# Sums of squares in two float32r products in place of two float32 products

## The chip, the cores and the metric

The kernel runs on one core of one Trainium2 chip. The metric is the device time of one execution in microseconds (us); lower is better. One profiled execution of the kernel before gives the rows that are quoted below.

## What is computed

A two-layer transformer block on 256 image tokens x and 256 context tokens (1024 features, float32), followed by a second block of two hybrid layers on x alone and a last norm. Cut to what matters here:

```python
def _rmsnorm(h, g):
    hf = h.astype(jnp.float32)
    hf = hf * lax.rsqrt(jnp.mean(hf * hf, axis=-1, keepdims=True) + NORM_EPS)
    return hf.astype(h.dtype) * g

def _modulate(h, shift, scale):
    return h * (1 + scale) + shift

# each sublayer of the first block, for x and for the context:
#   u = modulate(rmsnorm(h, g_pre), shift, scale)
#   y = sublayer(u)          # feed-forward, or an attention with its output product
#   h = h + factor * gate * rmsnorm(y, g_post)
# sublayers in order: ffn, differential attention, ffn | ffn, neighbourhood attention, ffn
```

So every sublayer needs two root-mean-squares per token for each half of the tokens: one of its output y, one of the new h. In the second block there are further norms over 256 features (MLA's c_q), over 128 features (c_kv, the heads of the attentions) and a last one over 1024.

## The kernel before

**Layout.** Features lie on the 128 partitions, tokens along the free dimension: h is a tensor of 128 partitions, 8 feature tiles, 512 tokens (x in 0 to 255, the context in 256 to 511). A sum over the features of a token is therefore a sum over 8 tiles and then over the partitions; the second one is a product with a matrix of ones on TensorE, which leaves the sum in every partition of a PSUM bank (tile `n`).

**Products.** Weights and activations are float32. `split` holds an operand as two float32r parts: ScalarE copies it into `hi`, VectorE subtracts that from it into `lo`. `mm3` makes each product in three passes of float32r. Weights arrive by DMA from the queue of SyncE (tile `raw`), are split (line 155 on ScalarE, line 156 on VectorE, tile `w`, 128x1024 each), and there are buffers for four split weights. TensorE's own work is one long queue of these passes.

**Sums of squares.** `Sums` (lines 54 to 81) takes four parts of 128 x 2 x 256 numbers. ScalarE squares a part (line 64, tile `r`, 128x512); VectorE adds parts 2 and 3 to part 1 (line 62, 128x512); with part 4, VectorE folds the sum of the first three and then part 4 itself to 128x256 (line 62, two instructions), and both 128x256 tensors go as a list to `rstd`. There (line 348, made by line 164 in `mm`) two float32 products with ones, 256 columns each, add them over the partitions. Then ScalarE takes the table's inverse root (line 353) and VectorE makes one Newton step of three instructions (lines 354 to 356). With `direct`, used where only x is left, the four squared parts go to TensorE in eight float32 products instead; the change leaves that as it is.

**Where the sums stand.** `link` (line 1348) joins two sublayers for one half of the tokens: `rstd` of y's sums, `add_normed` (lines 375 and 379: h += factor * y * r), `norm_r` (the sums of the new h), and `normed` (lines 413 to 421: the next input u, four tiles, each as hi and lo). For x, `link` stands behind the last products of x (`xdone`), and the context's last products of the same sublayer are there for TensorE meanwhile. For the context, `link` is the `mid` of the next sublayer, and TensorE has that sublayer's products of x meanwhile: two features (`AHEAD`) of the first feed-forward, five features of the second and third, or x's values and first queries and keys in an attention. There are four such joints with both halves (ffn to attention, attention to ffn, ffn to ffn, ffn to attention), which makes eight links of two sums each; before them stand the first norm of x (in `ada_first`) and of the context. Those are 18 sums that are not `direct`.

`rstd` is called with one 128x256 tensor in two more places of each hybrid layer (lines 1186 and 1195, the norms of c_q and c_kv; four in all): one float32 product each. With 512 columns it is called in the attentions, and that path stays.

**Order.** A scheduler orders the instructions of each engine beforehand: those that come first in the program go first, as soon as by its own estimate their operands and a buffer are there. On the chip each engine then runs its queue in that order and waits at the head of it. The 128x512 tiles of tag `r512` have two buffers.

Of the kernel before, what the change touches and what calls it, by code (L numbers as in the profile page):

```python
# [32 lines left out]
FA = 12  # L33
# [10 lines left out]
class Split:  # L44
    """A float32 operand held exactly as the sum of two float32r parts."""
# [8 lines left out]
class Sums:  # L54
    """sums of squares over the 1024 features of 256 tokens, from four parts [128, 2, 256]: the parts added
    up on the vector engine or, direct, on the tensor engine"""
# [3 lines left out]
    def add(self, x):  # L60
# [5 lines left out]
        if self.direct:  # L66
            if self.n == 1:
                self.acc = net.nps.tile([128, 512], F, name="n", tag="n")[:, :256]
            for t in range(2):
                net.mm(self.acc, net.ones, s[:, t], self.n + t == 1, self.n + t == 5)  # L70
        elif self.n == 1:
            self.acc = s
        elif self.n < 4:
            tt(self.acc, s)
        else:
            for x in (self.acc, s):
                tt(x[:, 0], x[:, 1])
            self.acc = [self.acc[:, 0], s[:, 0]]
# [5 lines left out]
class Net:  # L84
# [16 lines left out]
    @contextmanager  # L101
    def psum(self, **tags):
        """The PSUM banks of a phase: a number for each kind of use."""
        with ExitStack() as es:
            self.banks = self.pool(es, "ps" + "_".join(tags), 1, space=bass.MemoryType.PSUM)
            self.nbank = tags
            yield

    @contextmanager
    def space(self, name, n):  # L110
        """The 4 KiB tiles of a phase."""
# [4 lines left out]
    # ---- tiles  # L116
# [21 lines left out]
    # ---- weights: raw float32 from DRAM, then two float32r parts that sum to it  # L138
# [19 lines left out]
    # ---- products. A start clears the flags of its whole bank. Groups that share a bank are run one  # L158
    # after another (groups=0), or as one group (groups=n) whose first matmul alone has the start and
    # whose last alone the stop.  # L160
# [28 lines left out]
    # out += stat^T @ mov for every (out, mov), in three passes of float32r  # L189
# [12 lines left out]
    # ---- constants  # L202
    def setup(self):
        nc, I = self.nc, self.I
        self.ones = self.const([128, 128], "ones")
# [24 lines left out]
    # ---- modulation vectors: ada_w^T silu(c) + ada_b, as columns  # L230
    def ada_first(self):
        """The first layer's first scale and the last quarter of its shift on the tensor engine, the rest of
        the shift on the vector engine. Returns x's norm factors."""
# [45 lines left out]
    def ada_chunks(self, l, mods):  # L279
        """Thunks, one for each 128 values of modulation, and one for each vector that adds the bias."""  # L280
# [31 lines left out]
    def spread(self, thunks, steps):  # L312
        """An iterator: each next() runs its share of the thunks."""
# [11 lines left out]
    # ---- norm factors as columns  # L325
    def pre_cols(self, l, which, j):
        """(1 + scale) * g and shift of sublayer `which` (0, 1, 2) for half j."""
# [11 lines left out]
    # ---- 1 / sqrt(sum of squares / n + eps) in every partition: a table's value and one Newton step  # L339
    def rstd(self, ss, n, p=None):  # L340
        """ss: tensors whose sum is to be summed over the partitions, if p, that sum in PSUM, isn't given"""
        nc = self.nc
        if p is None:
            ss = ss if isinstance(ss, list) else [ss]
            w = ss[0].shape[-1]
            p = self.nps.tile([128, 512], F, name="n", tag="n")[:, :w]
            for i, x in enumerate(ss):
                self.mm(p, self.ones, x, i == 0, i == len(ss) - 1)
            v = ss[-1]
# [17 lines left out]
    def add_normed(self, y, r, cols, j):  # L367
        """h += cols * rmsnorm(y), y in two tiles [128, 4, 256]"""
# [12 lines left out]
    def table(self, x):  # L381
        """loads the table of the inverse root, once x is there"""
        self.nc.scalar.activation(self.col.tile([128, 1], F, name="tb", tag="tb", bufs=1), x, AF.Abs_reciprocal_sqrt)

    def new_u(self, n=2):
        """hi and lo of [1024, 256 n] features by tokens"""
# [16 lines left out]
    def normed(self, u, cols, shift, j, r=None, dve=False):  # L403
        """u = rmsnorm(h) * cols + shift in two parts"""
# [18 lines left out]
    def scaled(self, cols, shift=None):  # L423
        """h * cols of x in two parts, with shift's parts in the two columns that follow, if there is one, and
        the factors 1 / rms(h) of the tokens, along the free dimension in every partition"""
# [17 lines left out]
    def columns(self, r):  # L443
        """r as columns [128 tokens, 2]"""
# [7 lines left out]
    # ---- feed-forward  # L452
    def ffn(self, n, u, halves, mid, xdone, extra=(), r=None):
        """xdone(y) takes x's tiles of silu(a) * b @ w_out, then ctx's are worked out and returned.
        mid() is run when the work on x that needs nothing of ctx has been issued."""
# [51 lines left out]
        with self.space("ffn", 12):  # L507
# [19 lines left out]
            # the first FA features' share of y  # L527
# [11 lines left out]
            # the others', x before ctx  # L539
# [27 lines left out]
    # ---- shared parts of the mixers  # L567
# [10 lines left out]
    def projections(self, src, u, first):  # L578
        """starts the products of a mixer's queries (x's alone, if first is 1) and keys. The generator
        prefetches the weights of the next pair before it gives a pair's PSUM; the first pair's x comes  # L580
        apart, before ctx."""
# [20 lines left out]
    def v_tiles(self, src, u, mid, more):  # L602
        """token-major values [128 tokens, 1024] of the four token tiles, x's before mid()"""
# [31 lines left out]
    def out_proj(self, src, o, halves, xdone):  # L635
        """o(h, j) gives the pair [128, 256] of rows 128 h .. of the product's input for half j. The steps
        of the first quarter are given out, for use while o is still being made."""
# [52 lines left out]
    # ---- products of two 64-row operands, two to a tile: q = qh + ql stands on the rows of both halves,  # L690
    # so that one pass carries qh kh + ql kh and a second one qh kl
# [20 lines left out]
    # ---- differential attention  # L712
# [100 lines left out]
    # ---- neighbourhood attention (queries of x alone)  # L813
# [78 lines left out]
    # ---- the second block's layer  # L892
    def softmax_small(self, rows, scale, bias, n, e):
        """softmax over n keys of scale * (the scores in PSUM + bias), into e"""
# [8 lines left out]
    def causal_pair(self, q, k, v, scale, bias, gate, x):  # L903
        """x [128, 256] = gate * the two heads' causal attention, a head in each 64 partitions:
        q(j), k(j) feature-major, v(j, tt) token-major [128, 64], bias(j, qt) over 128 (qt + 1) keys"""
# [24 lines left out]
    def second_consts(self):  # L930
# [12 lines left out]
        # sel[:, k] spreads row k of every block of 16 rows over the block  # L943
# [31 lines left out]
    def gates(self, ba, abt):  # L975
        """beta and the log decay of GDN, token-major [128 tokens, 2 tiles, 4 heads]"""
# [11 lines left out]
        # log1p(e) = ln(w) + (e - (w - 1)) / w with w = 1 + e  # L988
# [12 lines left out]
    def delta_rule(self, prn, cw, gates, abt, others):  # L1001
        """Returns U and the causal q k matrix: o^T = U^T A, by the two tiles of tokens."""
# [22 lines left out]
        # decays between tokens j <= t, then the two triangular matrices, transposed: [j, t]  # L1025
# [36 lines left out]
        # inverses of the diagonal blocks, dd = (1 + N)^-1 and ee its transpose: blocks of 16 column by column,  # L1062
        # row k of a block spread over the block's rows by the tensor engine, then larger ones from pairs
# [45 lines left out]
        # values token-major, then both blocks' solutions  # L1109
# [20 lines left out]
    def rope_pe(self, x, n):  # L1130
        """in place on partitions 64 .. 95 of x [128, n, 256]"""
# [9 lines left out]
    def hybrid(self, l, scaled, prm3):  # L1141
# [35 lines left out]
        # MLA  # L1177
# [46 lines left out]
        # MoBA: the one block is the queries' own, so it is causal attention with the T5 bias  # L1224
# [13 lines left out]
        # GDN output  # L1238
# [24 lines left out]
        # h += the heads' product, the last heads after all others  # L1263
# [16 lines left out]
    # ---- the whole  # L1280
# [40 lines left out]
    def first_block(self, es, on, ada):  # L1321
# [10 lines left out]
        with self.psum(ab=3, ac=4):  # L1332
            # silu(c) along the free dimension, in every partition
# [214 lines left out]
```

## Time and profile before

| | |
|---|---|
| times of three runs | 2261.57, 2261.72, 2266.63 us (median 2261.72) |
| span of the profiled execution | 2263.0 us, from its first to its last instruction |
| TensorE matmuls (PE) | 2206.7 us busy, 98% of the span |
| TensorE weight loads (PEld) | 1884.7 us, 83% |
| VectorE (DVE) | 1590.9 us, 70% |
| ScalarE (ACT) | 1121.4 us, 50% |
| mean granted TensorE clock | 0.990 of full speed |

The span is the profiled execution's own time as far as the profile shows it: nothing of the execution lies outside it in the records. It is 1.3 us above the median of the runs. A matmul's record overlaps with the next one's, since they are pipelined; busy time is the union of the records. In a row of the timeline, equal instructions that follow one another are merged: the start, the time from the first start to the last end, what it is, and their count; in brackets, how long the engine was idle before and what ended that.

### The profile page before, as it was taken

Reading aid. Unit: us, or ns where it says so; the run is one execution under the profiler, and the core shown is the slowest. Engines: PE = TensorE matmul, PEld = TensorE weight load, DVE = VectorE, ACT = ScalarE, POOL = GpSimd, SP = SyncE. Lnnn points to the kernel's source line nnn. Section 1 sums busy time; section 2 is a strip of 40 time slices with the busy share of each in tenths; the row PEclk is TensorE's granted clock in tenths of the full one; section 3 lists DMA queues with packets and bytes.
Section 4 is the critical chain, followed back from the end, with each engine's and each line's share of the span. In section 5 each row is a group of like instructions: output and inputs, shape, how many; then the busy total and the mean of one; then the engine's idle time right before and its main releaser. Section 6 shows DMA issues by size and latency. Waiting matters only on the chain.

```text
span 2263.0 us, 33412 instructions
## 1 busy us (share of the span) xinstructions
PE 2206.7 (98%) x13010; PEld 1884.7 (83%) x13010; DVE 1590.9 (70%) x2899; ACT 1121.4 (50%) x1841; POOL 4.4 (0%) x29
## 2 busy tenths in 40 slices
PE   7999999999999999999999999999999989999998
PEld 4888889876679988889988889977789989888986
DVE  7876665868869876767854454956666568977985
ACT  4332224667768322235632233667654448547744
POOL 0000000000000000000000000000000000000000
PEclk9999999999989999999999999999999999999999
DMA  8555553421124755544554553432235553324321
GB/s 304 196 185 188 180 183 131 145 93 47 38 93 134 235 197 190 195 166 150 177 187 151 175 167 131 149 130 85 94 134 184 177 170 121 113 75 137 121 98 56
DMA packets 96164, 332.75 MB, mean 147 GB/s; under 512 B 12772, under 2 KB 15462, under 8 KB 96008
## 3 DMA queue, kind: packets, MB, share of 16 engines
q1 hardware_dynamic: 96008, 330.64, 43.0%
q8 instruction: 102, 1.67, 0.3%
q14 instruction: 54, 0.44, 0.1%
HBM read 329.55 MB, written 1.05 MB: 146 GB/s over the span
## 4 chain that ended last, share of the span: by engine, by line
PE 85%; DVE 7%; ACT 5%; DMA 1%; issue 1%; SPq 0%; DVEq 0%; ACTq 0%
PE ab L164 39%; PE ac L164 17%; PE ac L168 7%; PE pj L164 5%; PE ab L179 5%; PE gd L164 3%; PE n L164 3%; PE ab L168 2%; DVE w L156 1%; PE at L164 1%; ACT w L155 1%; PE gd L168 1%; DVE y L375 1%; PE pj L168 1%; DVE h L379 1%
## 5 line engine op out<-in xcount | busy, mean ns | idle before, releaser
L155 ACT ACTIVATE w<-raw 128x1024 fp32r<-128x1024 f32 x466 | 489.4, 1053 | 792.7 <-PE ab L164 271.9
L164 PE MATMUL ab<-u,w 128*128 128x512 f32 (+2 forms) x4320 | 876.2, 362 | 4.1 <-ACT u L438 4.1
L164 PEld LDWEIGHTS ab<-u,w 128*128 128x128 f32 x4320 | 727.2, 189 | 133.2 <-issue 5.1
L156 DVE TENSOR_TENSOR w<-raw,w 128x1024 fp32r<-128x1024 f32 x466 | 567.1, 1219 | 321.8 <-ACT w L155 314.9
L164 PE MATMUL ac<-b,w 128*128 128x512 f32 (+1 forms) x1152 | 235.9, 366 | 0.0
L164 PEld LDWEIGHTS ac<-b,w 128*128 128x128 f32 x1152 | 195.6, 188 | 39.6
L168 PE MATMUL ac<-b,w 128*128 128x256 f32 x1680 | 200.6, 280 | 0.0
L168 PEld LDWEIGHTS ac<-b,w 128*128 128x128 f32 x1680 | 198.4, 188 | 0.8
L164 PE MATMUL pj<-u,w 128*128 128x256 f32 (+1 forms) x1200 | 159.4, 289 | 5.6 <-ACT u L438 4.4
L293 DVE SCALAR_TENSOR_TENSOR ra<-ra,cb 128x1024 f32<-128x1024 f32 x130 | 158.2, 1221 | 5.5 <-ACT cb L1342 2.2
L164 PEld LDWEIGHTS pj<-u,w 128*128 128x128 f32 (+1 forms) x1200 | 148.7, 191 | 10.7 <-ACT u L438 5.0
L179 PE MATMUL ab<-u,w 128*128 128x256 f32 x1152 | 147.6, 290 | 7.6 <-ACT u L155 6.2
L179 PEld LDWEIGHTS ab<-u,w 128*128 128x128 f32 x1152 | 144.2, 197 | 9.2 <-ACT u L155 6.5
L293 DVE SCALAR_TENSOR_TENSOR c<-ra,cb 128x1024 f32<-128x1024 f32 x98 | 118.7, 1218 | 11.9 <-ACT cb L1342 6.4
L484 DVE TENSOR_TENSOR s<-s,ab 128x512 f32<-128x512 f32 (+1 forms) x78 | 47.0, 603 | 90.7 <-PE ab L164 90.2
L164 PE MATMUL ac<-w,u 128*128 128x512 f32 x384 | 90.4, 393 | 0.0
L164 PE MATMUL n<-r,ones 128*128 128x256 f32 (+1 forms) x216 | 77.4, 470 | 7.5 <-DVE r L62 3.1
L164 PEld LDWEIGHTS ac<-w,u 128*128 128x128 f32 x384 | 71.7, 188 | 15.4 <-DVE u L156 0.4
L155 ACT ACTIVATE b<-s 128x512 fp32r<-128x512 f32 (+1 forms) x100 | 53.5, 535 | 26.9 <-DVE s L484 19.8
L156 DVE TENSOR_TENSOR b<-s,b 128x512 fp32r<-128x512 f32 (+1 forms) x100 | 56.2, 562 | 3.1 <-ACT b L155 2.9
L164 PEld LDWEIGHTS n<-r,ones 128*128 128x128 f32 x216 | 37.7, 203 | 21.4 <-DVE r L62 9.4
L64 ACT ACTIVATE r<-h 128x512 f32<-128x512 f32 x56 | 35.1, 628 | 31.7 <-DVE h L379 10.7
(289 smaller groups left out, 2311.2 us busy)
## 6 DMA issues: line engine op xcount, KB each, us to landing
raw<-in_fin SPq DMA_DIRECT2D x194, 512.0 KB, 3.3
raw<-in_fout SPq DMA_DIRECT2D x112, 512.0 KB, 3.3
ra<-in_ada SPq DMA_DIRECT2D x72, 512.0 KB, 4.3
ra<-in_ada0r SPq DMA_DIRECT2D x58, 512.0 KB, 3.3
raw<-in_w SPq DMA_DIRECT2D x54, 512.0 KB, 3.3
raw<-in_da_qk SPq DMA_DIRECT2D x16, 512.0 KB, 3.2
raw<-in_na_qk SPq DMA_DIRECT2D x16, 512.0 KB, 3.3
raw<-in_w2o SPq DMA_DIRECT2D x16, 512.0 KB, 3.2
```

Of the source, the lines that this page charges most:

```text
L64: net.nc.scalar.activation(s, x, AF.Square)
L155: self.nc.scalar.activation(hi, x, AF.Copy)
L156: self.anchor = self.nc.vector.tensor_tensor(lo, x, hi.bitcast(F), op=OP.subtract).ins.name
L164: return mm(out, lhsT, rhs, start=start, stop=stop)
L168: ins = mm(out, lhsT, rhs, start=start and "first" not in bank, stop=stop and bank["done"] == n)
L179: ins = mm(out, lhsT, rhs, start=start, stop=stop)
L293: ins = nc.vector.scalar_tensor_tensor(junk, w, 1.0, self.cb[:, j], op0=OP.mult, op1=OP.mult, accum_out=self.mod[l][:, m, t, j:j + 1])
L375: ins = nc.vector.scalar_tensor_tensor(yy[:, t], yy[:, t], cols[:, k:k + 1], r, op0=OP.mult, op1=OP.mult)
L379: last = nc.vector.tensor_tensor(hh, hh, yy, op=OP.add).ins.name
L484: nc.vector.tensor_tensor(s, s, pb, op=OP.mult)
```

## The change

The second fold is replaced: VectorE adds everything up to one 128x256 tensor (one more instruction with part 3, and with part 4 the fold of part 4 and its addition to the sum). `rstd`, when it gets 256 columns, splits that tensor into a float32r `hi` (ScalarE) and `lo` (VectorE), in a tile of tag `r512`, and multiplies both with ones that are declared float32r. The `direct` sums and the 512-column ones are as before. Elsewhere the diff removes only comments.

```diff
@@ class Sums
         elif self.n == 1:
             self.acc = s
-        elif self.n < 4:
+        else:
+            if self.n == 4:
+                tt(s[:, 0], s[:, 1])
+                tt(self.acc[:, 0], s[:, 0])
+                self.acc = self.acc[:, 0]
+                return
             tt(self.acc, s)
-        else:
-            for x in (self.acc, s):
-                tt(x[:, 0], x[:, 1])
-            self.acc = [self.acc[:, 0], s[:, 0]]
+            if self.n == 3:
+                tt(self.acc[:, 0], self.acc[:, 1])
@@ def setup
-        self.ones = self.const([128, 128], "ones")
+        self.ones_r = self.cst.tile([128, 128], R, name="ones", tag="ones")
+        self.ones = self.ones_r.bitcast(F)
@@ def rstd
         if p is None:
-            ss = ss if isinstance(ss, list) else [ss]
-            w = ss[0].shape[-1]
+            w = ss.shape[-1]
             p = self.nps.tile([128, 512], F, name="n", tag="n")[:, :w]
-            for i, x in enumerate(ss):
-                self.mm(p, self.ones, x, i == 0, i == len(ss) - 1)
-            v = ss[-1]
+            if w == 256:
+                parts = self.tmp.tile([128, 2, w], R, name="r512", tag="r512", bufs=2)
+                self.split(ss, parts[:, 0], parts[:, 1])
+                for i in range(2):
+                    self.mm(p, self.ones_r, parts[:, i], i == 0, i == 1)
+            else:
+                self.mm(p, self.ones, ss, True, True)
+            v = ss
```

## Rows read from the trace of the kernel before

**Rows 1.** Page: busy time of each engine, and the chain that ended last, by engine.

```profile
PE 2206.7 (98%) x13010; PEld 1884.7 (83%) x13010; DVE 1590.9 (70%) x2899; ACT 1121.4 (50%) x1841; POOL 4.4 (0%) x29
...
PE 85%; DVE 7%; ACT 5%; DMA 1%; issue 1%; SPq 0%; DVEq 0%; ACTq 0%
```

**Rows 2.** Waits of PE: who ended them, total us, times, longest us.

```profile
PE ab L179 <- ACT u L155: 6.2, 2, 3.9
...
PE n L164 <- DVE r L62: 3.1, 6, 1.5
```

**Rows 3.** Groups by line, shapes apart: busy us, mean ns of one.

```profile
L168 PE MATMUL ac<-b,w 128*128 128x256 f32 x1680 | 200.6, 280 | 0.0
...
L164 PE MATMUL n<-r,ones 128*128 128x256 f32 x176 | 53.0, 419 | 7.5 <-DVE r L62 3.1 <-ACT r L64 2.9 <-ACT r L361 1.1
...
L156 DVE TENSOR_TENSOR b<-s,b 128x256 fp32r<-128x256 f32 x46 | 19.3, 419 | 3.1 <-ACT b L155 2.9
...
L155 ACT ACTIVATE b<-s 128x256 fp32r<-128x256 f32 x46 | 19.1, 415 | 21.0 <-DVE s L484 13.9 <-DVE s L493 7.1
```

**Rows 4.** Chain from 380 to 442 us (first joint): start, us, what.

```profile
384.94 0.67 PE n L164 x2
...
385.85 0.45 PE n L164 x2
...
386.32 0.49 ACT r L353
...
400.07 1.13 PE n L164 x4
```

**Rows 5.** Timeline, sums of y of x, first joint.

```profile
384.44 0.63 ACT L64 ACTIVATE r<-y 128x512 f32<-128x512 f32 x1 [1.22 <-DVE r L62]
...
385.10 0.42 DVE L62 TENSOR_TENSOR r<-r 128x256 f32<-128x256 f32 x1 [0.24 <-ACT r L64]
```

**Rows 6.** Timeline, sums of the new h of x, first joint.

```profile
399.60 0.76 DVE L62 TENSOR_TENSOR r<-r 128x256 f32<-128x256 f32 x2
...
400.27 2.36 DVE L156 TENSOR_TENSOR w<-raw,w 128x1024 fp32r<-128x1024 f32 x2
...
402.54 0.42 DVE L354 SCALAR_TENSOR_TENSOR r<-n,r 128x256 f32<-128x256 f32 x1
```

**Rows 7.** Timeline, first joint: u of x and of the context, and TensorE's next products.

```profile
409.14 0.68 DVE L156 TENSOR_TENSOR u<-c,u 128x512 fp32r<-128x512 f32 x1
...
413.53 3.14 PE L164 MATMUL ac<-w,u 128*128 128x512 f32 x13
...
437.56 6.15 PE L168 MATMUL ab<-u,w 128*128 128x256 f32 x50
...
440.67 0.69 DVE L156 TENSOR_TENSOR u<-c,u 128x512 fp32r<-128x512 f32 x1 [0.38 <-ACT u L155]
```

**Rows 8.** Timeline, links into the second and third feed-forward: products, and u's last tile.

```profile
699.44 2.66 PE L179 MATMUL ab<-u,w 128*128 128x256 f32 x21
...
729.34 0.69 DVE L156 TENSOR_TENSOR u<-c,u 128x512 fp32r<-128x512 f32 x1
...
1071.10 2.08 PE L179 MATMUL ab<-u,w 128*128 128x256 f32 x16
...
1071.83 0.68 DVE L156 TENSOR_TENSOR u<-c,u 128x512 fp32r<-128x512 f32 x1
...
1103.93 0.69 DVE L156 TENSOR_TENSOR u<-c,u 128x512 fp32r<-128x512 f32 x1
```

**Rows 9.** Timeline, the first two sums of the program.

```profile
21.94 0.70 PE L164 MATMUL n<-r,ones 128*128 128x256 f32 x2 [1.46 <-DVE r L62]
...
56.00 0.50 PE L179 MATMUL ab<-u,w 128*128 128x256 f32 x2 [2.28 <-ACT u L155]
```

**Rows 10.** Timeline, the norm of c_kv in the first hybrid layer.

```profile
1967.60 0.40 ACT L361 ACTIVATE r<-r 128x256 f32<-128x256 f32 x1
...
1968.05 0.70 PE L164 MATMUL n<-r,ones 128*128 128x256 f32 x2 [1.07 <-ACT r L361]
```

## Prediction

> **What bounds the kernel now.** The first look is at the page's busy times and at the chain that ended last: TensorE's matmuls are busy for 98% of the span, and the chain runs through PE for 85% of it [rows 1]. The second look is at what PE waits for. Waits for u, the input that a link makes, come to 6.2 us in two places, and waits of the norm's own products for VectorE's folds to 3.1 us in six [rows 2]. So over nearly all of the span TensorE's queue sets the time, and the chains of the links run beside it. The change takes work off that queue and puts more steps into those chains. The sum is therefore made link by link: the queue gets shorter, the chain beside it gets longer, and what counts is how much slack a link has.
>
> **What TensorE saves.** A float32r matmul of 256 columns costs 200.6 us / 1680 = 0.119 us of busy time; a float32 one is two records, 53.0 / 88 products = 0.60 us [rows 3]. That busy time has waits in it. The chain at the first joint is cleaner: the first product of a sum takes 0.67 us, the second, which follows without a wait, 0.45; a whole sum is 1.12 us, and the next one 1.13 [rows 4]. The 0.22 us between 0.67 and 0.45 are what a product loses when it has to wait for its operand and its weights can't be loaded ahead. After the change a sum is two float32r products, 2 x 0.119 = 0.24 us, plus that loss once or twice (`hi` and `lo` become ready at different times): 0.46 to 0.68. The saving is 0.44 to 0.66 us a sum; I take 0.55, with two losses half of the time. Sixteen sums in eight links: 8.8 us, and this is all that there is to win in the links: 7.0 to 10.6.
>
> **What the chain gains in length.** The tail of a sum becomes: fold of part 4 (as now), addition to the sum, copy on ScalarE, subtraction on VectorE, last product. Prices: the addition has the fold's shape, 0.42 us [rows 5]; copy 0.415 and subtraction 0.419 are rows of the same shapes and types in the feed-forward [rows 3]; each handover costs about 0.05, as between the square that ends at 385.07 and the fold at 385.10 [rows 5]. For y's sum of the first joint: fold 385.10 to 385.52, addition to 385.9, copy to 386.4, subtraction to 386.85, product (0.28 us from start to end [rows 3]) to 387.2, inverse root at 387.3 in place of 386.32 [rows 4]: 1.0 us later. For the new h's sum the two folds end at 400.36 [rows 6], and the four float32 records then take 1.13 us [rows 4], which the short products give back; on the other hand VectorE starts two splits of weights at 400.27, one 1.2 us long, and the Newton step starts only behind them at 402.54 [rows 6]. With copy and subtraction put among these splits I get about 0.5 us later; bounds 0.2 (the splits go behind) and 1.7 (the subtraction goes behind one more of them). A link of two sums so grows by 1.5 us. In the context's links VectorE and ScalarE are fuller and the Newton step already waits behind splits, which takes up a part: 1.2 us. The extra fold with part 3, one of 0.42 us, stands ahead of part 4's square and costs nothing, as long as VectorE waits for that square, as it does in [rows 5]; without this cover it is 0.4 more in a link. VectorE and ScalarE have room: 22 x 0.42 us of copies, and 40 x 0.42 us of VectorE's instructions, against 70% and 50% busy [rows 1].
>
> **Link by link.** While a link's chain grows, its cover on TensorE shrinks by 2 x 0.55 = 1.1 us. A link's change is then the larger of -1.1 (still hidden) and growth minus slack (now the chain decides).
> - x into the two attentions: u's first tile is whole at 409.82, TensorE comes to it at 413.53 [rows 7]. Slack 3.7 against 1.5 + 1.1: hidden, -1.1 each, -2.2.
> - x into the second and third feed-forward: TensorE starts at 1071.10, needs the last of four tiles 18 products of 0.12 us later, at 1073.3, and has it at 1072.51 [rows 8]: slack 0.75, so between -1.1 and +0.75. The tile is late because a weight split runs ahead of it on VectorE, which can as well go behind; I take -0.5 each, -1.0.
> - the context into the two attentions: first tile whole at 441.36; TensorE has products of x from 437.56, 48 of 0.12 us, until 443.3 [rows 7]. Slack 1.9 against 1.2 + 1.1: -0.7 each, -1.4.
> - the context into the second feed-forward: five features of x are 240 products of 0.12 us from 699.44, with two sums of 1.1 to 1.6 us between them: until about 731, and the last tile is needed 2.2 us later, at 733; it is whole at 730.03 [rows 8]. Slack 3: -1.1.
> - the context into the third: the same count from 1071.10 gives 1102.2 and 1104.4; the last tile is whole at 1104.62 [rows 8]. Slack none: +1.2.
>
> Together -4.5 us of the 8.8.
>
> **The first two sums.** After the first one TensorE waits for the folds already (1.46 us), and the path goes on over the modulation's products; I put it at 0, with bounds -0.6 and +1.5, the latter if `lo` waits behind one of the 1.2 us instructions that fill VectorE there. After the second, the context's first norm, TensorE runs dry and waits 2.28 us for u [rows 9]: growth is paid there in full, 0 to 1.0, I take +0.5.
>
> **The four sums of the second block.** One float32 product of 0.45 becomes two of 0.12: -0.2 each at the norm of c_q. At c_kv the queue stands still already: the product at 1968.05 waited 1.07 us for a square that ends at 1968.00 [rows 10]; now copy and subtraction stand between (0.84 + 0.1, less 0.2): +0.7, and +0.35 in the second layer, where I expect half. Sum +0.65; bounds -0.8 and +2.
>
> **Sum.** -4.5 + 0 + 0.5 + 0.65 = -3.35 us: the span goes from 2263.0 to 2259.7. The span is 1.3 us above the median of the runs, so the median goes from 2261.7 to 2258.4.
>
> **A page against this.** PE's 98% are the first reason here, and PE's records overlap. The Trainium skill (Perfetto Trace Analysis, Identifying the Most-Contended Engine) says that matmul busy time doesn't tell how near TensorE is to its limit, and wants weight loads' busy share instead, which is 83% here [rows 1]. By that rule some of what the products give back would be idle time already, and the sum would be the chain's growth alone, rival 3. The rows of this case speak against it within the links: 1680 products of one group cost 0.119 us each with no idle time before them [rows 3].
>
> **Rivals.**
> 1. *All of it stays hidden.* The scheduler moves splits behind the chain, or takes other products first, so that no link shows: 16 x 0.55 to 0.66, with 3 us of waits of the norm's products [rows 2] partly gone too: -9 to -12 us, 2251. For it: no link after the first waits visibly now. Against it: slack of 0 to 0.75 us in three links [rows 8].
> 2. *The norm's products hold up the queue: slower.* TensorE's order is fixed beforehand, and a product that waits holds all behind it. The scheduler's estimate must now be right over two more engines. If `lo` falls behind one more weight split on VectorE (2.36 us for two [rows 6]) than the estimate has it, TensorE stands for 1.2 us in each sum: 18 x (1.2 - 0.55) = +12 us, 2274. It decides from 0.55 us of additional standing per sum on, and shows beyond the measurement from 0.93. For it: in six places the products wait today already, 1.5 us at worst [rows 2]. Against it: the other five share 1.6 us.
> 3. *TensorE's records overstate it, and no time comes back*, in the links: chain growth in the dry places alone, +0.5 + 0.65 = +1.2 us, 2263.
>
> **How the numbers follow.** A measurement of this kernel can tell about 0.3%, 6.8 us, from no change. Forecast 0.52 and rival 3 with 0.04 end within it: same 0.56. Rival 1 has 0.30, and ends beyond it: faster 0.30. Rival 2 has 0.14: slower. The range reaches down to rival 1's best end, 2250, which is also the bound of all unknown costs at their low ends, and up to 2267, the forecast with all of them at their high ends (links +4, the rest +3.5 over what is taken). The likeliest case's own range is 2255 to 2264.
>
> **What the next profile would show.** Products n in 256-column shape fall from 176 records [rows 3] to 140: 96 float32 records of the six direct sums stay, and 44 of float32r come, each near 0.12 us of busy time. PE's busy time falls by 9 to 13 us; if it falls by less, the first step is wrong. VectorE's folds show 18 more instructions and the splits 22 more. Waits of PE for u appear at the links into the third feed-forward and, smaller, into the attentions; if there are none, rival 1 holds. Waits of `n` for a split beyond 10 us in total would be rival 2. The prediction fails if the scheduler puts large parts of the order elsewhere.

## The result and the profile after

The changed kernel takes 2294.22 us (median of 4 runs, 2292.07 to 2295.35) beside 2263.83 us for the kernel before (4 runs, 2261.57 to 2266.63): a ratio of 1.0129, 95% interval 1.0116 to 1.0141. It is slower by 30 us where 3.3 us less were forecast. The profiled execution took 2295.35 us, its span is 2292.9 us. Lines have moved: the fold and the addition are L62, splits L158 (ScalarE's copy) and L159 (VectorE's subtraction), the root L361, Newton L362 to L364.

The page of the changed kernel, busy times and chain, beside [rows 1]:

```profile
PE 2208.1 (96%) x12974; PEld 1886.1 (82%) x12974; DVE 1606.3 (70%) x2939; ACT 1132.2 (49%) x1865; POOL 4.4 (0%) x29
...
PE 85%; DVE 7%; ACT 5%; issue 1%; DMA 1%; SPq 0%; DVEq 0%; ACTq 0%
```

PE has 36 records fewer and is busy 1.4 us longer. Span less busy time of PE was 2263.0 - 2206.7 = 56.3 us and is 84.8: 28.5 of the 29.9 us by which the span grew are new idle time of TensorE. What ended it, in the waits of PE (total us, times, longest), beside [rows 2]:

```profile
PE ab L182 <- ACT u L158: 11.9, 4, 5.8
PE ab L182 <- DVE w L159: 9.2, 3, 5.0
PE ab L171 <- ACT u L158: 7.5, 2, 4.5
...
PE n L167 <- ACT r L158: 3.3, 5, 2.2
...
PE n L167 <- ACT r L64: 2.7, 3, 1.6
...
PE n L167 <- DVE r L159: 1.1, 3, 0.4
```

The waits are for u, the end of a link (the first and third line, with 6.2 us in [rows 2]), and for weights whose split is late (the second line, 0.2 us in the kernel before). The norm's own products wait 7.1 us in all, not more than before. Their group (shapes apart: busy us, mean ns, idle before), beside [rows 3]:

```profile
L167 PE MATMUL n<-r,ones 128*128 128x256 f32 x140 | 42.5, 400 | 7.4 <-ACT r L158 3.3 <-ACT r L64 2.7 <-DVE r L159 1.1
```

140 records, as the change has it, and 10.5 us less than the 53.0 before. That PE is busy longer all the same is put down to the clock: its mean grant is 0.983 of full speed after and 0.990 before, 0.017 x 2292.9 less 0.010 x 2263.0 = 16 us of full-speed time. Stretches of the changed kernel with new waits, and those behind them, show it (start and end, length, busy of PE, PEld, VectorE, ScalarE and GpSimd, granted clock, DMA):

```profile
700.00:706.00 6.00, 2.84 (x22) 2.43 (x21) 5.58 (x9) 6.00 (x13) 0.00 (x0) 0.99 0.11 28
706.00:709.00 3.00, 3.00 (x16) 3.00 (x16) 2.07 (x4) 3.00 (x8) 0.00 (x0) 0.50 0.34 132
...
1490.00:1494.60 4.60, 0.15 (x2) 0.05 (x1) 3.83 (x8) 2.47 (x6) 0.00 (x0) 0.98 0.31 110
1494.60:1501.20 6.60, 6.46 (x19) 5.26 (x20) 2.70 (x4) 4.03 (x8) 0.00 (x0) 0.50 0.00 0
...
441.00:454.00 13.00, 9.53 (x62) 8.31 (x61) 7.39 (x13) 7.58 (x15) 0.00 (x0) 1.00 0.00 1
454.00:630.00 176.00, 172.08 (x722) 122.64 (x720) 137.25 (x277) 125.87 (x244) 0.00 (x0) 1.00 0.17 60
```

In the first and third stretch TensorE waits for 3.2 and 4.5 us; in the second and fourth it works at 0.50, which is 1.2 GHz, so these two waits cost more time behind them. Not every new wait does: in the fifth, at the first joint, TensorE waits for 3.5 us, and neither there nor in the 176 us that follow does the grant fall.

Where a link became longer is seen in the timeline. The new h's sum at the first joint, beside [rows 6] (start, length, engine, line, operation):

```profile
404.34 0.42 DVE L62 TENSOR_TENSOR r<-r,r 128x256 f32<-128x256 f32 x1
404.67 2.35 DVE L159 TENSOR_TENSOR w<-raw,w 128x1024 fp32r<-128x1024 f32 x2
404.85 0.42 ACT L158 ACTIVATE r<-r 128x256 fp32r<-128x256 f32 x1 [0.17 <-DVE r L62]
...
406.94 0.42 DVE L159 TENSOR_TENSOR r<-r,r 128x256 fp32r<-128x256 f32 x1
407.28 2.35 DVE L159 TENSOR_TENSOR w<-raw,w 128x1024 fp32r<-128x1024 f32 x2
...
407.41 0.39 PE L167 MATMUL n<-r,ones 128*128 128x256 f32 x1 [0.38 <-DVE r L159]
...
407.84 0.48 ACT L361 ACTIVATE r<-n,eps 128x256 f32<-128x256 f32 x1 [0.67 <-PE n L167]
...
409.55 0.42 DVE L362 SCALAR_TENSOR_TENSOR r<-n,r 128x256 f32<-128x256 f32 x1
```

The high part is there at 405.27. The low part needs 0.42 us and nothing else, but stands on VectorE behind two splits of weights and starts at 406.94. The root is there at 408.32; two more splits stand in front of the Newton step. Before, one such pair stood in the whole tail [rows 6]; now there are two.

At the link into context's second feed-forward ScalarE adds to it:

```profile
711.14 0.43 DVE L62 TENSOR_TENSOR r<-r,r 128x256 f32<-128x256 f32 x1
711.67 0.41 ACT L158 ACTIVATE r<-r 128x256 fp32r<-128x256 f32 x1
711.80 1.23 DVE L159 TENSOR_TENSOR w<-raw,w 128x1024 fp32r<-128x1024 f32 x1 [0.24 <-ACT w L158]
712.95 0.42 DVE L159 TENSOR_TENSOR r<-r,r 128x256 fp32r<-128x256 f32 x1
...
714.67 1.28 ACT L491 ACT_TABLE_LOAD   x1
...
716.37 1.28 ACT L361 ACT_TABLE_LOAD   x1
...
717.66 0.47 ACT L361 ACTIVATE r<-n,eps 128x256 f32<-128x256 f32 x1
```

The later sum lets a Silu of x's features go first, and with it the tables change twice before the root. From the end of y's last square to the end of u's last tile, read from the timelines of both kernels, the links take:

| link into | before | after | more |
|---|---|---|---|
| first attention, x / context | 29.9 / 28.7 | 33.6 / 30.6 | 3.7 / 2.0 |
| second feed-forward, x / context | 26.3 / 27.4 | 30.2 / 36.7 | 3.9 / 9.3 |
| third feed-forward, x / context | 29.9 / 30.2 | 33.6 / 36.6 | 3.7 / 6.4 |
| second attention, x / context | 29.9 / 30.1 | 33.6 / 31.9 | 3.7 / 1.8 |

Together 34.5 us. The tail of a sum, from its last square's end to the end of the Newton steps, grew from 4.52 to 7.12 us, mean over the links' 16 sums. Events of the changed kernel are late by 2.5 us ahead of the first of these joints and by 4.7 behind it; by 3.1 ahead of the second, since the attention between them has 10 us at a grant of 0.50 in place of 14; by 11.4, 19.8 and 29.0 us behind the others, and by 29.9 at the end. The joints cost 2.1, 8.3, 8.4 and 9.3 us, while their links grew by 5.7, 13.2, 10.1 and 5.5. So the growth of the links doesn't give the time by itself: the fourth joint grew as little as the first, but two stretches at 0.50 follow (the one from 1494.6 above and one of 6.8 us from 1538.7), and none follows the first.

### The profile page after: what moved, and what is told of

It reads as the page before. It is cut to its first block, busy times and chain, and to the rows that moved or that the text cites. A ratio compares the mean times of both kernels' runs of the same rounds, so it can differ in the third digit from the quotient of the medians.

```text
span 2292.9 us, 33447 instructions
## 1 busy us (share of the span) xinstructions
PE 2208.1 (96%) x12974; PEld 1886.1 (82%) x12974; DVE 1606.3 (70%) x2939; ACT 1132.2 (49%) x1865; POOL 4.4 (0%) x29
## 3 DMA queue, kind: packets, MB, share of 16 engines
HBM read 329.55 MB, written 1.05 MB: 144 GB/s over the span
## 4 chain that ended last, share of the span: by engine, by line
PE 85%; DVE 7%; ACT 5%; issue 1%; DMA 1%; SPq 0%; DVEq 0%; ACTq 0%
PE ab L167 38%; PE ac L167 17%; PE ac L171 8%; PE pj L167 5%; PE ab L182 5%; PE gd L167 3%; PE n L167 2%; PE ab L171 2%; PE at L167 1%; DVE w L159 1%; ACT w L158 1%; PE gd L171 1%; PE pj L171 1%; DVE y L383 1%; DVE r L62 1%
## 5 line engine op out<-in xcount | busy, mean ns | idle before, releaser
L158 ACT ACTIVATE w<-raw 128x1024 fp32r<-128x1024 f32 x466 | 489.6, 1053 | 798.8 <-PE ab L167 271.3
L159 DVE TENSOR_TENSOR w<-raw,w 128x1024 fp32r<-128x1024 f32 x466 | 567.5, 1221 | 333.2 <-ACT w L158 327.1
L182 PE MATMUL ab<-u,w 128*128 128x256 f32 x1152 | 153.0, 296 | 24.2 <-ACT u L158 11.9
L167 PEld LDWEIGHTS pj<-u,w 128*128 128x128 f32 (+1 forms) x1200 | 147.8, 190 | 10.5 <-ACT u L446 5.0
L167 PE MATMUL n<-r,ones 128*128 128x256 f32 (+1 forms) x180 | 66.3, 462 | 7.4 <-ACT r L158 3.3
L158 ACT ACTIVATE b<-s 128x512 fp32r<-128x512 f32 (+1 forms) x100 | 53.5, 535 | 26.7 <-DVE s L492 19.6
L159 DVE TENSOR_TENSOR b<-s,b 128x512 fp32r<-128x512 f32 (+1 forms) x100 | 56.3, 563 | 2.5 <-ACT b L158 2.4
```

Source lines behind the costliest of these rows:

```text
L158: self.nc.scalar.activation(hi, x, AF.Copy)
L159: self.anchor = self.nc.vector.tensor_tensor(lo, x, hi.bitcast(F), op=OP.subtract).ins.name
L167: return mm(out, lhsT, rhs, start=start, stop=stop)
L182: ins = mm(out, lhsT, rhs, start=start, stop=stop)
```

## The experiments

The first theory was that each handover between VectorE and ScalarE leaves a gap in the order that a split of a weight (1.05 us on ScalarE, 1.22 on VectorE) fills. "Tails" and "links" below are measured as above; ratios are to the kernel before on the same chip.

**One product, no split.** The addition of the change alone.

```diff
-                self.split(ss, parts[:, 0], parts[:, 1])
-                for i in range(2):
-                    self.mm(p, self.ones_r, parts[:, i], i == 0, i == 1)
+            self.mm(p, self.ones, ss, True, True)
```

> One summed tensor, added on VectorE as in the changed kernel, but given to one plain float32 product with ones; no split into two parts. Theory (each handover of the split lets a split of a weight in front of it in the fixed order, and the links outgrow their cover): the two handovers are gone, only one VectorE addition more than before stands in the chain, so 2255 to 2265 us, and no wait of TensorE for the split of a weight at the link into context's feed-forward. Rival (VectorE's additional addition is what lengthens the chain): stays at 2285 us or above. Rival (the first sum's split pins the shift's chunks behind it): nothing else changes, so only the start's part of the loss comes back, about 2 us, and 2290 us.

2262.56 us, 0.9991 (0.9982 to 1.0000). The addition, with one product less per sum, costs nothing that can be measured: links +7.6 us, 0.47 a sum, about its own duration; PE's busy time 2198.2, 8.5 less than before. The loss comes with the split.

**High part alone.**

```diff
-                self.split(ss, parts[:, 0], parts[:, 1])
-                for i in range(2): ...
+                nc.scalar.activation(parts[:, 0], ss, AF.Copy)
+                self.mm(p, self.ones_r, parts[:, 0], True, True)
```

> As the changed kernel, but only the high part is made (by ScalarE) and multiplied; the low part, its subtraction on VectorE and its product are left out, so the sums have float32r's precision alone. Theory (handovers): one of the two added handovers is left, VectorE to ScalarE, so about half of the loss comes back: 2270 to 2284 us. Rival (the whole loss is the copy's place behind a weight's copy on ScalarE): 2290 us or above. Rival (it is the subtraction's place behind a weight's subtraction on VectorE): 2265 us or below.

2267.35 us, 1.0011 (1.0000 to 1.0022). Links +9.4 us. The copy on ScalarE costs some 5 us against one product (2 by the run with the high part twice, below), not half of 30. The theory had the parts wrong: nearly all comes with the low part, 34.5 - 9.4 = 25 us of the links' growth.

**Second product, or subtraction?** The high part multiplied twice; and the low part made, but not multiplied.

```diff
-                    self.mm(p, self.ones_r, parts[:, i], i == 0, i == 1)
+                    self.mm(p, self.ones_r, parts[:, 0], i == 0, i == 1)   # and no subtraction
```
```diff
-                for i in range(2):
-                    self.mm(p, self.ones_r, parts[:, i], i == 0, i == 1)
+                self.mm(p, self.ones_r, parts[:, 0], True, True)           # subtraction stays
```

> As the changed kernel, but no low part is made: the high part is multiplied twice, so the sum that comes out is double and without its low part. Both products are there, the subtraction is not. Theory (the subtraction on VectorE, which stands behind splits of weights, is the cost): as with the high part alone, 2265 to 2272 us. Rival (the second product in TensorE's queue is the cost): 2285 us or above.

> As the changed kernel, but the low part is made and not multiplied: left out of the sum is its product alone. The subtraction stands in VectorE's queue, and nothing in the chain waits for it by its data. Theory (it costs as a step that the chain waits for): 2266 to 2275 us. Rival (it costs as time and place in VectorE's queue, whoever waits): 2285 us or above.

Twice the high part: 2264.36 us, 0.9998 (0.9988 to 1.0007). The second product is free. The low part unused: 2272.66 us, 1.0035 (1.0024 to 1.0047). So of the changed kernel's 30 us the subtraction costs 5 (against the high part alone) to 8 (against the high part twice) as work on VectorE whose result nothing waits for, and some 21 more once the chain waits for it. The split's tile takes one of the two `r512` buffers in both runs too, so that isn't the loss. PE is busy 2195.2 and 2194.8 us, 11.5 and 11.9 less than before: the saving is there. It is there in time as well, as the first product of the first attention's probabilities with its values shows, in the kernel before, the changed one and the one with the high part twice:

```profile
489.95 1.99 PE L179 MATMUL ab<-pT,v 128*128 128x256 f32 x8 [0.36 <-ACT pT L786]
...
494.62 1.56 PE L182 MATMUL ab<-pT,v 128*128 128x256 f32 x6 [0.36 <-ACT pT L794]
...
489.01 1.99 PE L182 MATMUL ab<-pT,v 128*128 128x256 f32 x8 [0.36 <-ACT pT L794]
```

With the high part twice, events are late by 0.9 us ahead of the first joint (y's last square ends at 385.99, 385.07 before) and early by 0.9 behind it: four sums gave back 1.9 us, 0.47 each. Timeline of the unused low part at the new h's sum of the first joint:

```profile
403.60 0.42 DVE L62 TENSOR_TENSOR r<-r,r 128x256 f32<-128x256 f32 x1
...
403.94 2.36 DVE L159 TENSOR_TENSOR w<-raw,w 128x1024 fp32r<-128x1024 f32 x2
404.51 0.40 ACT L158 ACTIVATE r<-r 128x256 fp32r<-128x256 f32 x1
...
404.99 0.36 PE L167 MATMUL n<-r,ones 128*128 128x256 f32 x1
...
405.39 0.47 ACT L360 ACTIVATE r<-n,eps 128x256 f32<-128x256 f32 x1 [0.48 <-PE n L167]
...
406.21 0.42 DVE L159 TENSOR_TENSOR r<-r,r 128x256 fp32r<-128x256 f32 x1
...
406.74 0.42 DVE L361 SCALAR_TENSOR_TENSOR r<-n,r 128x256 f32<-128x256 f32 x1
```

Copy, product and root run beside the two splits, which delay one step of VectorE, as before the change. In the changed kernel product and root come behind the subtraction, and the Newton step needs a second place in VectorE's order.

**High part on VectorE too.**

```diff
-                self.split(ss, parts[:, 0], parts[:, 1])
+                nc.vector.tensor_copy(parts[:, 0], ss)
+                nc.vector.tensor_tensor(parts[:, 1], ss, parts[:, 0].bitcast(F), op=OP.subtract)
```

> As the changed kernel, but VectorE makes the high part too (a copy in place of ScalarE's), so that addition, high part and low part follow one another on one engine. Theory (handovers): most of the loss comes back, since ScalarE's queue is no longer passed in the middle of the chain: 2262 to 2278 us. Rival (serial work on VectorE is the loss): the copy moves to VectorE, which is no shorter, so 2290 us or above. Rival (the two float32r products wait in TensorE's queue in front of the weights' products): unchanged at 2294 us.

2288.78 us, 1.0110 (1.0094 to 1.0125): 5 us back, near the rival. A change of engine is not needed for a split of a weight to come between: at the first joint's new h the copy and the subtraction each have one in front. Nor does the number of VectorE's steps alone set the cost: this kernel has one more of them in each tail than the changed kernel and is faster (links +26.2 us in place of 34.5).

**Low part on GpSimd.**

```diff
+                nc.scalar.activation(parts[:, 0], ss, AF.Copy)
+                ... nc.gpsimd.tensor_tensor(parts[:, 1], ss, parts[:, 0].bitcast(F), op=OP.subtract)
```

> As the changed kernel, but GpSimd makes the low part (the subtraction of 128x256), so that it stands in no queue with the weights' subtractions; high part and both products stay. Theory (place behind a weight's subtraction on VectorE): although GpSimd is slower by itself, most of the 27 us between the changed kernel and the one without the low part comes back, 2265 to 2280 us. Rival (two products of which the second waits are the loss, wherever the low part is made): 2290 us or above. Rival (GpSimd's subtraction is itself longer than the place behind a weight): 2294 us or above with tails longer than 6 us.

2296.21 us, 1.0140 (1.0126 to 1.0154): nothing comes back, and the timeline says why.

```profile
407.42 3.49 DVE L159 TENSOR_TENSOR w<-raw,w 128x1024 fp32r<-128x1024 f32 x3
407.59 0.42 ACT L352 ACTIVATE r<-r 128x256 fp32r<-128x256 f32 x1 [0.27 <-DVE r L62]
408.08 3.40 POOL L353 TENSOR_TENSOR r<-r,r 128x256 fp32r<-128x256 f32 x1 [15.62 <-ACT r L352]
...
411.54 0.38 PE L167 MATMUL n<-r,ones 128*128 128x256 f32 x1 [2.74 <-POOL r L353]
...
445.77 0.73 POOL L353 TENSOR_TENSOR r<-r,r 128x256 fp32r<-128x256 f32 x1 [16.32 <-ACT r L352]
```

Beside three splits on VectorE the operation takes 3.40 us and ends behind them; where VectorE has none it takes 0.73. So the low part waits for the weights on GpSimd as well. The Trainium skill (SBUF — State Buffer, SBUF: two separate sides) says that VectorE, reading two operands in SBUF, and a GpSimd operation that reads SBUF exclude each other at a shared port; the trace agrees with these two durations.

**Weights behind the sum.** Weights that are issued later in the program wait for the sum's high part on ScalarE and its low part on VectorE: for both sums of a link; for y's sum alone; and, in the kernel before, for root and last Newton step of both.

```diff
+        if self.pins:                  # in weight(): a, b are the copy and the subtraction
+            self.after(a, self.pins[0])
+            self.after(b, self.pins[1])
```

> As the changed kernel, nothing left out, but the order is written so that a weight which is split later in the program has its copy behind the sum's high part on ScalarE and its subtraction behind the sum's low part on VectorE. Theory (the loss is the 1.05 us copies and 1.22 us subtractions of weights that the order puts in front of the sum's two added steps): the tails of the sums fall to 2.3 to 2.8 us each and most of the 30 us comes back, 2258 to 2272 us. Rival (the sum's own added steps, with their serial time, cost the loss): tails as before this edit, 2288 us or above. Rival (the weights are late instead): tails are short, but TensorE then waits for weights, 2275 us or above with its long waits on the split of a weight.

> As the changed kernel, nothing left out, but only the sum of y holds back the weights that are issued after it (their copies behind its high part, their subtractions behind its low part); the sum of the new h does not. The earlier run held weights back behind both sums of a link, and TensorE then waited about 9 us for them in front of the second sum's product. Theory (weights' subtractions in front of the sum's added steps are the loss): y's tails fall from 5.7 and 8.7 us to 4.2 to 4.5 us, and part of the loss comes back, 2272 to 2288 us. Rival (VectorE has no room at all, so whatever is put behind the sum is late for TensorE): 2294 us or above, with waits of TensorE for a weight's split.

> The kernel before the change, with the same order of weights behind root and last Newton step. It shows what the order alone is worth without the change: if it is 2250 to 2258 us, the changed kernel with the same order has to be compared with this one and not with the kernel before, and the change itself costs their difference; if it is 2264 us or above, the order helps the changed kernel only because it repairs what the change made longer.

2377.74 us, 1.0509 (1.0494 to 1.0525); 2303.49 us, 1.0172 (1.0157 to 1.0188); 2399.75 us, 1.0612 (1.0595 to 1.0630). The changed kernel with its weights behind root and last Newton step of both sums, expected at 2252 to 2268 us, took 2406.81 us, 1.0638 (1.0622 to 1.0654). With the weights behind the split of both sums the links are shorter than before the change by 0.9 us together, and TensorE stands at the sums' products, which its order now has in front of the late weights:

```profile
PE n L173 <- ACT r L162: 87.0, 14, 11.3
```

So the splits in front of the sum's steps are no idle filling: TensorE needs these weights during the link. Both demands meet on VectorE. These edits hold back every later weight; an order that holds back only some wasn't run.

**Silu behind the root.**

```diff
+                if self.root:          # the latest sum's root
+                    self.after(ins, self.root)
```

> As the changed kernel, but the Silu of a feed-forward that is issued later in the program stands behind the root of the sum before it on ScalarE, so that no table load of Silu and back comes in front of a root. Theory (two table loads of 1.28 us in front of the root are part of the loss at the links into context's feed-forwards): the tails of context's sum into the second and third feed-forward fall by about 3 us each, 2282 to 2290 us. Rival (Silu stands there because the sum is late, and would be idle time anyway): 2292 us or above.

2309.47 us, 1.0205 (1.0190 to 1.0221). Both links get shorter (31.8 and 32.3 us in place of 36.7 and 36.6), and the time grows by a further 17 us (0.0205 - 0.0129 of 2263): TensorE needs the Silu too. It waits 9.6 us for products of it in two places, and 16.1 us at the sums:

```profile
PE n L168 <- ACT r L159: 16.1, 6, 6.5
...
PE ab L183 <- DVE s L497: 9.6, 2, 4.8
```

**Two more operations off the chain**, in the kernel before.

```diff
+            if n == D:
+                for _ in range(2):
+                    nc.vector.tensor_reduce(self.junk, ss[0], axis=AX.X, op=OP.max)
```

> The kernel before, with two more VectorE operations of 128x256 (0.42 us each, a maximum that nobody reads) at each sum over the 1024 features, off the chain: no later step waits for them, but they stand in VectorE's queue. They are as much VectorE time as the change adds (an addition and a subtraction). Theory (VectorE is full in the links, so its time there is what counts): eight links times 1.7 us, 13 us, of which a part is hidden: 2270 to 2282 us. Rival (only the chain's own steps and handovers count): 2263 to 2267 us.

2269.98 us, 1.0026 (1.0017 to 1.0036): between the two expectations, 6 us. The links grew by 1.2 us together, so VectorE's time alone makes no longer link; but in one link weights come late (waits of 1.10 and 1.75 us there and the late sums' products), and that keeps:

```profile
718.60 6.02 PE L179 MATMUL ab<-u,w 128*128 128x256 f32 x48 [1.10 <-DVE w L156]
...
729.52 0.79 PE L179 MATMUL ab<-u,w 128*128 128x256 f32 x4 [1.75 <-ACT w L155]
```

Little room was left. Over the four joints of the kernel before VectorE is busy for 86 to 89%, and in the two stretches shown (columns as in the windows above) for 92 and 98%, against 70% over the span [rows 1]:

```profile
404.00:420.00 16.00, 16.00 (x111) 14.52 (x110) 14.69 (x21) 13.10 (x22) 0.00 (x0) 1.00 0.54 179
421.00:434.00 13.00, 13.00 (x60) 10.74 (x59) 12.72 (x21) 7.74 (x11) 0.00 (x0) 1.00 0.56 202
```

**Where it is lost.** The new form in x's links alone, and in context's links alone (`Sums` and `rstd` take a flag).

```diff
+        ss = [Sums(self, halves == 1, j == 0) for j in range(halves)]     # the other: j == 1
```

> The changed form in x's links alone (four links, eight sums); context's links, the first two sums and c_kv's as before. In the changed kernel x's links grew by 3.7 to 3.9 us each, 15 us together, context's by 19.5 us. Theory (each link's growth goes into the time by itself): some 15 us less 4 us that TensorE saves, so 2272 to 2278 us. Rival (only context's links cost time, x's have cover): 2258 to 2265 us. Rival (the links' losses are not additive, one displaces the next): 2285 us or above.

> The changed form in context's links alone; x's links, the first two sums and c_kv's as before. x's links alone cost 9 us of the 30. If the losses add up, context's links give some 18 to 20 us: 2280 to 2285 us. If each link's growth comes from the one before it (x's late link pushes work into context's), 2275 us or below. If the link has its slack already used up by the addition, above 2288 us.

2273.60 us, 1.0038 (1.0024 to 1.0052), and 2274.96 us, 1.0042 (1.0026 to 1.0059): 9 and 10 us by the ratios. The links grew by 9.0 us (x's by 14.9, while the context's became 5.8 shorter) and 17.6 us. With about 2.5 us at the start and 1 in the second block that makes some 22 of 30. By this subtraction, with about 3 us of uncertainty in each ratio, the rest appears only where both links of a joint have the new form.

**The modulation's order.** The sum's split sets `anchor`, behind which later chunks of the modulation stand.

```diff
+                anchor = self.anchor
                 self.split(ss, parts[:, 0], parts[:, 1])
+                self.anchor = anchor
```

> As the changed kernel, but the split of a sum is no longer the point behind which later chunks of the modulation are ordered. If that side effect costs the start its time, about 2 to 3 us come back, nearly all before 70 us of the span: 2291 to 2292 us; the links are unchanged. If the side effect reached the other links as well, more than 5 us come back. If the start is late for the split itself, nothing changes: 2294 us.

2294.36 us, 1.0137 (1.0119 to 1.0154). Nothing comes back; this suspicion falls.

**More cover.** Six in place of five feature tiles of x ahead of context's link, in the changed kernel and in the kernel before.

```diff
-AHEAD = (2, 5, 5, 0)
+AHEAD = (2, 6, 6, 0)
```

> As the changed kernel, with six in place of five feature tiles of x ahead of context's link in the second and third feed-forward, so that TensorE has one tile more (about 5 us) to do while the link runs, but splits two weights twice more for each. Theory (cover): TensorE's waits of 5.0 and 3.7 us in these two links go, with the half-rate stretches behind them, 2280 to 2288 us. Rival (VectorE is full and the additional weights go through it): no gain, 2292 us or above.

> The kernel before with six feature tiles of x ahead of context's link, for comparison with the same edit of the changed kernel. Its links into context's feed-forwards leave TensorE waiting 0.1 to 0.2 us only, so cover can give nothing: 2263 to 2266 us by either theory; above that if the additional weights cost VectorE time in the links.

2292.45 us, 1.0120 (1.0105 to 1.0135), and 2273.04 us, 1.0035 (1.0024 to 1.0045). The waits at the two links stay (4.98 and 3.68 us), so they were for weights and not for want of x's tiles. The kernel before loses 8 us by the ratio with the same edit, with no link longer: its weights are split twice for one tile more.

**The version that the runs point to**, one product in the links, the rest as before: the links' sums are added up as in the changed kernel, and `rstd` is that of the kernel before (cut; the first sums and the four of the second block don't have the flag `new`).

```diff
+        elif not self.new:
+            ...                            # as before
+        else:
+            if self.n == 4:
+                tt(s[:, 0], s[:, 1])
+                tt(self.acc[:, 0], s[:, 0])
+                self.acc = self.acc[:, 0]
+                return
+            tt(self.acc, s)
+            if self.n == 3:
+                tt(self.acc[:, 0], self.acc[:, 1])
```

> The kernel before with one edit in the links alone: the two tensors of squares are added on VectorE and one float32 product replaces two; the first two sums and c_kv's are as before. Theory (the saving of TensorE's time is there, the split eats it): one added step of 0.46 us in each tail, 16 products of 0.3 us less, and without the 2.6 us that the run with one product lost before 65 us of the span: 2257 to 2262 us, under the kernel before. Rival (an addition on VectorE eats as much as the product gives): 2264 us or above.

2262.82 us, 0.9994 (0.9985 to 1.0003): just above the expected range, and not measurably better than the kernel before.

## Why the prediction was wrong

- **What TensorE saves** held. 140 records of n came out; the products of a link's sum are busy for 0.71 us in place of 1.26 (means of 16), which is the 0.55 taken. Where the chain doesn't wait for the subtraction (the runs with the high part twice and with the low part unused) PE's busy time falls by 11.5 and 11.9 us, inside the 9 to 13. In the changed kernel it rises by 1.4, as the clock's 16 us hide the saving.
- **What the chain gains in length** is the step that failed. It priced each added step at its own duration and 0.05 us of handover: y's sum +1.0, the new h's +0.5 with bounds 0.2 and 1.7, a link +1.5 or +1.2. Where VectorE has no weight to split in between, that is right: y's tail of x into the second feed-forward went from 3.10 to 4.22 us. Elsewhere the subtraction, on which product and root now wait, takes a place behind one or two splits, and the Newton step a second one: the new h's tail of x at the first joint went from 5.20 to 8.86, the mean tail grew by 2.6 us, and the links by 34.5 us in place of 4 x 1.5 + 4 x 1.2 = 10.8. [Rows 6] showed the pair of splits in front of the Newton step; the prediction counted it as cover that the new steps fit into, and it was the price of one more step.
- **Room on VectorE** ("70% busy") was read over the whole span. In the joints it was 86 to 89%, in stretches 92 and 98%, and what stands in the queue there is needed by TensorE at once: the runs that pushed the weights or the Silu back lost more.
- **Link by link** failed with that. The slacks of 0 to 3.7 us were not tested by themselves: growth of 1.8 to 9.3 us went beyond most of them, and TensorE waits. The context's link into the third feed-forward, with slack "none", grew by 6.4 us, but the one into the second, with slack 3, by 9.3; two table loads of 1.28 us stand in its tail, which the prediction did not think of. Some waits are paid again at the clock of 1.2 GHz behind them, which no term of the sum held.
- **The first two sums** came to about 2.5 us, the sum of their upper bounds (+0.5 taken). **The four sums of the second block** came to 0.9 us, 0.65 forecast.
- **Rivals.** Rival 2 had the cause in part (the low part behind one more split) and the sign, but another place: the norm's products wait no longer than before, 7.1 us in both, TensorE waits for u and for weights. Rival 1 is out by the time. Rival 3, that no time comes back, is out by the first joint of the run with the high part twice, where 1.9 us came back over four sums.

What stays open: how the subtraction's 21 us as a step of the chain divide between the delay of u, the weights that become late behind it, and the clock; and why a wait at the fourth joint was followed by 1.2 GHz and one at the first was not. Taking the splits away from the chain without making them late for TensorE was not achieved.

## What to carry to other kernels

A step added to a dependent chain can cost a place in its engine's order and not only its duration: the subtraction's 0.42 us became 1.6 (25 us over 16 sums), as 1.22 us splits of weights take turns with it, while the addition cost 0.47, about its duration. Read an engine's busy share in the stage that the chain runs in, and ask who needs the work that shares the queue; here TensorE needed both. Work removed from the engine that bounds the kernel is worth nothing if the chain that feeds it becomes longer by more than its slack; time the cheap half of such a change (here the addition) alone, which may bring nothing either, as it did here (0.9994).

## What the hardware showed unexpectedly

GpSimd's subtraction of 128x256 took 0.73 us beside an idle VectorE and 3.40 us beside three splits. New idle time of TensorE of a few us (3.2 us between 700 and 706, 4.5 from 1490 on) was followed by a stretch at 1.2 GHz, 3.0 and 6.6 us in the windows shown; 3.5 us between 441 and 454 were not.
